# The first half of each stage-end norm in three operations per tile, from PSUM, with query norms ahead of the search

## The chip, the cores and the metric

The kernel runs on one core of a Trainium2 chip. The metric is the time of one execution on the device, in microseconds, as the median of several runs. The engines named below are TensorE (PE, with PEld for its weight loads), VectorE (DVE), ScalarE (ACT), GpSimd (POOL) and SyncE (SP, which only issues transfers here).

## What is computed

Two layers of a trunk, for a prompt of 512 tokens and 8 samples of 4 tokens, 544 columns in all, with 1024 channels:

```python
h  = rmsnorm(x, norm1) * (1 + sc1) + sh1          # shift, scale and gate: silu(c) @ w_ada + b_ada
q, k, v, qi, ki, wi, pool_u, z, xbc, dt, gates = split(h @ w_in)
q = rope(rmsnorm(q, q_norm), pos)                 # 16 heads of 64: the query norms
# attention over the 256 keys with the best indexer scores (the search), pooling, state-space scan
x = x + g1 * (merged @ w_out)
h2 = rmsnorm(x, norm2) * (1 + sc2) + sh2
a, g = split(causal_dwconv3(h2 @ ffn_up))
x = x + g2 * ((silu(g) * a) @ ffn_down)
```

The prompt has one shift and scale per channel, each sample its own. All in fp32.

## The kernel before

Channels lie on the 128 partitions (8 tiles `x[k]` of 128 x 544), tokens in the free dimension, in two halves of 272 columns; the samples are the last 32 columns of the second half. Each fp32 product runs as three fp32r products: weights and activations are split into a rounded part and a rest (`wh` and `wl`, `hh` and `hl`), and `wh*hh`, `wh*hl` and `wl*hh` are added up in PSUM. `weights` (L348) loads a 512 KB tile to `raw` over SP's queue, casts it to `wh` on ACT and subtracts to `wl` on VectorE (L357), all with a raised priority. `raw` has four buffers, `wh` and `wl` three each. `gemm` (L360) makes one such product with 48 matmuls (L371).

`gemm2` (L375) makes two products half by half (L388): both sources for the first 272 columns, then both for the rest. It is used at the three stage ends (layer 0's output projection to its FFN, layer 0's FFN to layer 1's projection, layer 1's output projection to its FFN). There `gemm_norm` (L472) makes the last two output tiles and calls `norm` after each half, while PE goes on to the other half; the next stage begins with `gemm2` as well, so that it can start on the half that is ready.

A norm half (`norm`, L397) squares on ACT (L428), adds up on VectorE (L430), takes the mean over channels with matmuls (L459), then eleven small VectorE operations (`newton`, L303, and two that add eps) for the inverse root `rstdh`; six matmuls (L468) spread it over the partitions, and a copy brings it to SBUF as `rb`. Then per tile: `hn = x * rb` (L434), `hn * gm + shift` (L444, ACT Identity), the cast to `hh` and the subtraction to `hl` (L452). For the first tile but one, the multiply and the last subtraction are on POOL (the sites nm1 and nl1), for the last tile the cast is on VectorE (nh7). In the second half the samples take two more POOL operations per tile (L449, L450).

Work of other chains is issued in steps: `pump` takes from each lane as many generator steps as its rate, once in each `gemm` and twice in `gemm2`. Lane a is `ada` (L246), the product of silu(c) with w_ada: in the start-up for layer 0's first third, in layer 0's pooling branch for the rest, and in layer 0's FFN for layer 1. Lane t is the search (`topk1`, L856), pairs of MAX8 and MATCH_REPLACE8 on VectorE. In `attention` (L1301) `qnorm` takes the inverse root of the query norms for two groups of four tiles, into the halves of `rq`; `qbc` (L1369) spreads a half for the sample tokens, and PE turns it in L1374. A planner (TileContext) orders each engine's instructions before the run, by their place in the program, the raised priorities and its own timing; the order is then fixed, and each engine follows its own list.

Of the kernel before, what the change touches and what calls it, by code (L numbers as in the profile page):

```python
# [23 lines left out]
F32 = mybir.dt.float32  # L24
F32R = mybir.dt.float32r
BF16 = mybir.dt.bfloat16
I32 = mybir.dt.int32
AF = mybir.ActivationFunctionType
OP = mybir.AluOpType
# [7 lines left out]
HC = T // 2  # L37
# [9 lines left out]
WPRI = 300  # L47
# [43 lines left out]
W_UP = 127  # L91
# [12 lines left out]
class Prog:  # L104
# [134 lines left out]
    def ada(self, l, s, first=False):  # L239

        nc, a = self.nc, self.a
        par, mod, _ = self.par[l]
        m0 = 16 * s
        pick = lambda x: x.rearrange("p (h c t) n -> p c h t n", h=2, c=4)
        dst = pick(mod[:, m0:m0 + 16, :])
        bias = par[:, P_BADA + m0:P_BADA + m0 + 16].rearrange("p (h c t) -> p c h t", h=2, c=4)  # L246
        turn = None
        for c in range(4):
            ps = self.P("ada1")
            for pair in range(2):  # L250
                raws = []
                for z in (2 * pair, 2 * pair + 1):
                    with self.tc.high_priority(offset=WPRI):
                        raw = self.wr.tile([128, 1024], F32, name="raw", tag="raw")
                        nc.sync.dma_start(raw, a["w_ada"][l, s, 4 * c + z])
                    raws.append(raw)
                    if z % 2 == 0:
                        yield

                prods = []  # L260
                for k4 in range(4):
                    prods.append(nc.tensor.matmul(ps[32 * k4:32 * k4 + 32, :], self.sc[:, 4 * pair + k4, :],
                                     raws[k4 // 2][:, (k4 % 2) * 512:(k4 % 2) * 512 + 512],
                                     start=(pair == 0), stop=(pair == 1)))
                if pair == 0:
                    if turn:
                        turn(prods[-1].ins)
                        turn = None
                    yield
            if turn:  # L270
                turn(prods[-1].ins)
            row = self.t("adarow")
            self.copy("ada2", row[:, :512], ps)
            turn = self.ada_turn(row, dst[:, c], bias[:, c], first)
            if first or c == 3:
                turn(None)
                turn = None
            yield
# [68 lines left out]

    def weights(self, src, n):  # L348
        nc = self.nc
        z = self.nw = (self.nw + 1) % 4  # L350
        with self.tc.high_priority(offset=WPRI):
            raw = self.wr.tile([128, 1024], F32, name="raw", tag="raw")
            nc.sync.dma_start(raw[:, :n], src)
            wh = self.wh.tile([128, 1024], F32R, name="wh", tag="wh")
            wl = self.wh.tile([128, 1024], F32R, name="wl", tag="wl")
            self.copy("weights2", wh[:, :n], raw[:, :n])
            self.last_wl = self.E("weights1").tensor_tensor(wl[:, :n], raw[:, :n], wh[:, :n].bitcast(F32), op=OP.subtract).ins  # L357
        return wh, wl
# [15 lines left out]

    def gemm2(self, srcs, rhs, done=None):  # L375

# [3 lines left out]
        K = len(rhs)  # L380
        ws, self.pre = self.pre or [self.weights(src, K * 128) for src in srcs], None
        os_ = [self.G() for _ in srcs]
# [14 lines left out]
    def norm(self, l, second, c, st):  # L397
        if c == 0:
            for k in range(0, 8, 2):
                self.norm_gm(l, second, st, k)  # L400
        self.norm_stats(c, st, self.nc.gpsimd)
        for k in range(8):
            self.norm_apply(l, second, c, st, k)

# [8 lines left out]

    def norm_stats(self, c, st, eng):
        nc = self.nc
# [10 lines left out]
        for k in range(8):  # L426
            q = st["q"][k] if k else sq[0]
            nc.scalar.activation(q[:, cs], self.x[k][:, cs], AF.Square)  # L428
            if k:
                (nc.vector if k >= NV else eng).tensor_tensor(sq[k % 2][:, cs], sq[1 - k % 2][:, cs], q[:, cs],  # L430
                                                              op=OP.add)
        self.norm_half(sq[1], c, rb)
        for k in range(8):
# [19 lines left out]

    def norm_half(self, sq, c, rb):
        nc = self.nc
# [11 lines left out]
        for i, (t0, w) in enumerate(blocks):  # L467
            nc.tensor.matmul(o[:, t0:t0 + w], r[:w, i:i + 1].to_broadcast([w, 128]), self.ident[:w, :w],  # L468
                             start=True, stop=True)
        self.copy("norm_half3", rb[:, c * HC:c * HC + HC], o[:, :HC])  # L470

# [117 lines left out]
    def project(self):  # L589
        nc, a, l = self.nc, self.a, self.l  # L590
        par, mod, _ = self.par[l]
        h = self.h
        o, ok = self.gemm2([self.w(l, W_KI), self.w(l, W_K)], h)
        kd, self.ki = self.t("kd"), self.t("ki")
# [706 lines left out]
    def attention(self):  # L1301
# [29 lines left out]
        def qnorm(sqs, c0):  # L1331
            mk = yield from self.ssq(sqs, "mq")
            self.newton(mk, self.s([128, 5, 8], "rsq_u8"), rq[:, :, c0:c0 + 8])
            yield
# [33 lines left out]
        for p in range(2):  # L1368
            self.E("attention7").tensor_copy(bc[p][:32, :512].rearrange("p (i e d) -> p i e d", i=4, e=2),  # L1369
                                  rq[:32, 4, 8 * p:8 * p + 8].rearrange("p (i e) -> p i e", e=2)[:, :, :, None]  # L1370
# [239 lines left out]
    def ffn(self):  # L1610
# [7 lines left out]
        for ci, n in enumerate(CH):  # L1618
            fs = []
            for jj in range(n):  # L1620
# [8 lines left out]
                if j == 0:  # L1629
                    o, o2 = self.gemm2([self.w(l, W_UP), self.w(l, W_UP + 1)], h)  # L1630
                else:
                    o = self.gemm(self.w(l, W_UP + 2 * j), h)
# [200 lines left out]
```

## Time and profile before

| what | value |
| --- | --- |
| median of 3 runs | 3163.01 us (3154.23, 3163.01, 3165.09) |
| the profiled execution | 3159.91 us, of which the span is 3158.1 us |
| mean granted clock of TensorE | 0.980 |
| PE busy | 3037.2 us (96%) |
| VectorE busy | 2235.4 us (71%) |
| ACT busy | 1261.9 us (40%) |
| POOL busy | 881.0 us (28%) |

Times in rows are microseconds from the span's start, unless they are marked ns. An idle time stands in brackets with what ended it. A row can stand for several instructions in a row of the same kind (x7). L numbers are lines of the kernel before. Matmul ends are modelled, and neighbours in one engine overlap a little, so that durations add up to somewhat more than the time they take.

### The profile page before, as it was taken

The numbers are of one execution on the slowest core, as the hardware profiler recorded it, in microseconds if no ns is written. First come the engines' busy times: TensorE is split into PE (matmuls) and PEld (weight loads), VectorE is DVE, ScalarE is ACT, GpSimd is POOL, SyncE is SP. The second block draws the span as 40 slices with busy tenths as digits, with TensorE's granted clock in tenths as the row PEclk, the third lists the DMA queues.
The fourth block names the chain that finished last, engine by engine and source line by source line (L and its number), as shares of the span: only waits on it lengthen the run. The fifth ranks groups of instructions, "written<-read, shape, count | busy, mean of one in ns | idle before, by whom it ended". The sixth has DMA issues, their size and how long they took to land. (4 is left out here: it accounts for less than half of the span.)

```text
span 3158.1 us, 62620 instructions
## 1 busy us (share of the span) xinstructions
PE 3037.2 (96%) x24136; PEld 2791.9 (88%) x24136; DVE 2235.4 (71%) x4879; ACT 1261.9 (40%) x2240; POOL 881.0 (28%) x1273
## 2 busy tenths in 40 slices
PE   7999999999999999999989999999999899999999
PEld 4987998999986789998989878989999857899999
DVE  5687878679988656454566878786799885564554
ACT  4344443333336534343443344343333364342432
POOL 1363445521121003111223635455211110121211
PEclk9999999999999999999999999999999899999999
DMA  6332332345543443545333323223333244333322
GB/s 234 107 110 75 113 95 99 113 137 185 190 125 122 162 143 102 162 153 170 94 117 107 107 78 116 93 90 123 99 132 116 79 136 152 98 90 90 86 97 76
DMA packets 303100, 376.81 MB, mean 119 GB/s; under 512 B 177362, under 2 KB 186930, under 8 KB 302802
## 3 DMA queue, kind: packets, MB, share of 16 engines
q1 hardware_dynamic: 116514, 315.94, 29.7%
q10 hardware_dynamic: 181216, 42.05, 6.6%
q0 software_dynamic: 5072, 14.83, 1.3%
q8 instruction: 190, 3.11, 0.4%
q14 instruction: 108, 0.88, 0.1%
HBM read 330.34 MB, written 33.79 MB: 115 GB/s over the span
## 5 line engine op out<-in xcount | busy, mean ns | idle before, releaser
L371 PE MATMUL psg<-hh,wh 128*128 128x272 f32 x4064 | 859.0, 291 | 9.1 <-ACT cacc L894 4.9
L177 ACT ACTIVATE wh<-raw 128x1024 fp32r<-128x1024 f32 (+2 forms) x434 | 425.0, 980 | 1107.1 <-PE psg L371 752.1
L371 PE MATMUL psg<-hl,wh 128*128 128x272 f32 x4064 | 850.0, 289 | 0.0
L371 PE MATMUL psg<-hh,wl 128*128 128x272 f32 x4064 | 847.6, 290 | 0.0
L357 DVE TENSOR_TENSOR wl<-raw,wh 128x1024 fp32r<-128x1024 f32 (+2 forms) x434 | 509.5, 1174 | 334.2 <-ACT wh L177 329.6
L371 PEld LDWEIGHTS psg<-hh,wh 128*128 128x128 f32 x4064 | 642.8, 190 | 35.4 <-issue 14.0
L371 PEld LDWEIGHTS psg<-hh,wl 128*128 128x128 f32 x4064 | 640.4, 189 | 9.8 <-issue 7.2
L371 PEld LDWEIGHTS psg<-hl,wh 128*128 128x128 f32 x4064 | 640.4, 190 | 6.8 <-issue 4.7
L896 POOL COPY sti<-cu 128x32 f32<-128x32 f32 x136 | 85.4, 628 | 522.7 <-ACT cu L177 522.5
L901 DVE SCALAR_TENSOR_TENSOR cacc<-cu,half,cacc 128x511 f32<-128x511 f32 x144 | 137.4, 954 | 5.9 <-ACT cacc L894 4.9
L910 ACT ACTIVATE th<-cacc 128x544 f32<-128x544 f32 x92 | 60.4, 656 | 199.7 <-DVE cacc L904 179.8
L371 PE MATMUL psg<-fh,wh 128*128 128x272 f32 x648 | 133.9, 290 | 2.6 <-DVE resid L495 2.6
L371 PE MATMUL psg<-fl,wh 128*128 128x272 f32 x648 | 133.7, 288 | 0.0
L371 PE MATMUL psg<-fh,wl 128*128 128x272 f32 x648 | 133.6, 288 | 0.0
L489 DVE SCALAR_TENSOR_TENSOR x<-psg,mod,x 128x272 f32<-128x272 f32 x64 | 32.0, 499 | 140.5 <-PE psg L371 131.4
L371 PE MATMUL psg<-oh,wl 128*128 128x272 f32 x512 | 110.1, 291 | 0.0
L371 PE MATMUL psg<-ol,wh 128*128 128x272 f32 x512 | 109.4, 291 | 0.0
L371 PE MATMUL psg<-oh,wh 128*128 128x272 f32 x512 | 109.3, 292 | 0.0
L371 PEld LDWEIGHTS psg<-fh,wh 128*128 128x128 f32 x648 | 100.8, 188 | 8.6 <-PE psg L371 3.4
L1638 POOL TENSOR_TENSOR cacc<-cacc 128x544 f32<-128x544 f32 x44 | 62.2, 1414 | 154.5 <-DVE cacc L911 154.5
L1041 POOL TENSOR_TENSOR seg<-seg,cb 128x512 f32<-128x512 f32 x64 | 89.9, 1407 | 52.5 <-ACT seg L1040 39.3
L911 DVE SCALAR_TENSOR_TENSOR cacc<-th,cacc 128x544 f32<-128x544 f32 x92 | 72.8, 792 | 42.7 <-ACT th L910 42.5
(481 smaller groups left out, 6180.0 us busy)
## 6 DMA issues: line engine op xcount, KB each, us to landing
raw<-wk SPq DMA_DIRECT2D x326, 512.0 KB, 3.3
raw<-w_ada SPq DMA_DIRECT2D x96, 512.0 KB, 4.3
h<-h SPq DMA_DIRECT2D x64, 256.0 KB, 4.5
raw<-wk SPq DMA_DIRECT2D x64, 256.0 KB, 2.8
o_ssds<-hn ACTq DMA_DIRECT2D x64, 256.0 KB, 2.1
raw<-wd SPq DMA_DIRECT2D x32, 448.0 KB, 3.4
kvr<-ckv SPq DMA_DIRECT2D x48, 256.0 KB, 4.0
kvw<-ckv SPq DMA_DIRECT2D x48, 256.0 KB, 3.9
```

Of the source, the lines that this page charges most:

```text
L177: self.nc.scalar.activation(out, src, AF.Copy)
L357: self.last_wl = self.E("weights1").tensor_tensor(wl[:, :n], raw[:, :n], wh[:, :n].bitcast(F32), op=OP.subtract).ins
L371: nc.tensor.matmul(o[:, c, :HC], w[:, k * 128:(k + 1) * 128], x[:, c * HC:(c + 1) * HC], start=(k == 0 and first), stop=(k == K - 1 and last))
L489: self.E("resid1").scalar_tensor_tensor(x[:, :HC], o[:, 0, :HC], g[:, 0:1], x[:, :HC], op0=OP.mult, op1=OP.add)
L896: self.E("conv1").tensor_copy(st[:, i, :, W - 1:], new)
L901: self.E("conv3").scalar_tensor_tensor(acc[:, s:512], u[:, :512 - s], wc, acc[:, s:512], op0=OP.mult, op1=OP.add)
L910: nc.scalar.activation(th, acc, AF.Tanh)
L911: self.E("silu21").scalar_tensor_tensor(acc, th, 1.0, acc, op0=OP.add, op1=OP.mult)
L1041: self.E("ssd_chain5").tensor_tensor(d[:, :512], d[:, :512], cb[:, :512], op=OP.mult)
L1638: self.E("ffn3").tensor_tensor(s_, s_, aa, op=OP.mult)
```

## The change

Four edits:

- `norm`, first half only: `norm_half` no longer copies to `rb` but returns the PSUM tile, the multiplies of `norm_stats` are left out, and `norm_direct` makes each tile in three operations: `u = x * gm * o` on VectorE from PSUM, `hi = u + shift` on ACT, `lo = (u + shift) - hi` on VectorE. It does the same for all eight tiles.
- `weights` can put the subtraction to `wl` on another engine; the two products that begin layer 1's projection and each FFN use POOL. (In layer 0's projection these weights are prepared earlier, on VectorE as before.)
- `ada` loads both tiles of a pair and only then yields, so that their matmuls come one step later than both loads.
- In `attention`, `newton` for the query norms and the copy to `qbc` have their priority raised by 600 places (twice WPRI).

```diff
@@ ada
                         nc.sync.dma_start(raw, a["w_ada"][l, s, 4 * c + z])
                     raws.append(raw)
-                    if z % 2 == 0:
-                        yield
+                yield
 
@@ weights, gemm2
-    def weights(self, src, n):
+    def weights(self, src, n, eng=None):
...
             self.copy("weights2", wh[:, :n], raw[:, :n])
-            self.last_wl = self.E("weights1").tensor_tensor(wl[:, :n], raw[:, :n], wh[:, :n].bitcast(F32), op=OP.subtract).ins
+            eng = eng or self.nc.vector
+            if eng is self.nc.gpsimd:
+                eng.tensor_tensor(wl[:, :n], raw[:, :n], wh[:, :n].bitcast(F32), op=OP.subtract)
+                return wh, wl
+            self.last_wl = eng.tensor_tensor(wl[:, :n], raw[:, :n], wh[:, :n].bitcast(F32), op=OP.subtract).ins
...
-        ws, self.pre = self.pre or [self.weights(src, K * 128) for src in srcs], None
+        ws, self.pre = self.pre or [self.weights(src, K * 128, eng) for src in srcs], None
@@ norm
-        self.norm_stats(c, st, self.nc.gpsimd)
+        o = self.norm_stats(c, st, self.nc.gpsimd, not c)
         for k in range(8):
-            self.norm_apply(l, second, c, st, k)
+            if c:
+                self.norm_apply(l, second, c, st, k)
+                continue
+            self.norm_direct(l, second, c, st, k, o)
+
+    def norm_direct(self, l, second, c, st, k, o):
...
+        sh = mod[:, b + k, 0:1]
+        nc.vector.scalar_tensor_tensor(u[:, ps], x[:, ps], gm[:, k, 0:1], o[:, :t1 - t0], op0=OP.mult, op1=OP.mult)
+        nc.scalar.activation(hi.bitcast(F32R)[:, ps], u[:, ps], AF.Identity, bias=sh)
+        nc.vector.scalar_tensor_tensor(lo.bitcast(F32R)[:, ps], u[:, ps], sh, hi[:, ps], op0=OP.add, op1=OP.subtract)
@@ norm_stats, norm_half
-        self.norm_half(sq[1], c, rb)
+        o = self.norm_half(sq[1], c, rb, direct)
+        if direct:
+            return o
...
-        self.copy("norm_half3", rb[:, c * HC:c * HC + HC], o[:, :HC])
+        if not direct:
+            self.copy("norm_half3", rb[:, c * HC:c * HC + HC], o[:, :HC])
+        return o
@@ project
-        o, ok = self.gemm2([self.w(l, W_KI), self.w(l, W_K)], h)
+        o, ok = self.gemm2([self.w(l, W_KI), self.w(l, W_K)], h, eng=nc.gpsimd)
@@ attention
             mk = yield from self.ssq(sqs, "mq")
-            self.newton(mk, self.s([128, 5, 8], "rsq_u8"), rq[:, :, c0:c0 + 8])
+            with self.tc.high_priority(offset=2 * WPRI):
+                self.newton(mk, self.s([128, 5, 8], "rsq_u8"), rq[:, :, c0:c0 + 8])
...
-            self.E("attention7").tensor_copy(bc[p][:32, :512].rearrange("p (i e d) -> p i e d", i=4, e=2),
+            with self.tc.high_priority(offset=2 * WPRI):
+                self.E("attention7").tensor_copy(bc[p][:32, :512].rearrange("p (i e d) -> p i e d", i=4, e=2),
@@ ffn
-                    o, o2 = self.gemm2([self.w(l, W_UP), self.w(l, W_UP + 1)], h)
+                    o, o2 = self.gemm2([self.w(l, W_UP), self.w(l, W_UP + 1)], h, eng=nc.gpsimd)
```

## Rows read from the trace of the kernel before

**Rows 1.** Part 1 of the page: busy time, share of the span, instructions.

```profile
PE 3037.2 (96%) x24136; PEld 2791.9 (88%) x24136; DVE 2235.4 (71%) x4879; ACT 1261.9 (40%) x2240; POOL 881.0 (28%) x1273
```

**Rows 2.** Waits of PE: who waited for whom; us in total, times, longest.

```profile
PE psb L1374 <- DVE qbc L1369: 9.5, 2, 8.6
PE psb L262 <- DMA raw<-w_ada: 9.0, 6, 4.5
PE psa L468 <- DVE rstdh L311: 8.5, 4, 3.8
```

**Rows 3.** The same list for the first 70 us alone.

```profile
PE psb L262 <- DMA raw<-w_ada: 2.9, 3, 2.1
```

**Rows 4.** Timeline of PE, second stage end: start, duration, operation, idle before.

```profile
1622.88 1.35 PE L468 MATMUL psa<-cst,rstdh 128*128 128x128 f32 x6 [3.80 <-DVE rstdh L311]
...
1627.33 0.82 PE L388 MATMUL psg<-hh,wh 128*128 128x272 f32 x2 [2.01 <-ACT hh L177]
```

**Rows 5.** Windows there: busy us per engine (instructions), granted clock, DMA share, GB/s.

```profile
1632.00:1636.00 4.00, 4.00 (x17) 3.83 (x17) 3.22 (x8) 1.47 (x4) 2.32 (x6) 0.50 0.00 0
...
1640.00:1644.00 4.00, 4.00 (x35) 4.00 (x34) 2.06 (x6) 0.88 (x3) 0.72 (x4) 1.00 0.00 0
```

**Rows 6.** Timeline of VectorE, second stage end, in order of time.

```profile
1616.81 1.23 DVE L357 TENSOR_TENSOR wl<-raw,wh 128x1024 fp32r<-128x1024 f32 x1 [0.22 <-ACT wh L177]
...
1620.12 1.23 DVE L357 TENSOR_TENSOR wl<-raw,wh 128x1024 fp32r<-128x1024 f32 x1
...
1622.66 0.16 DVE L311 SCALAR_TENSOR_TENSOR rstdh<-rsq_u,rstdh 128x3 f32<-128x3 f32 x1
1624.27 0.44 DVE L173 COPY rb<-psa 128x272 f32<-128x272 f32 x1 [1.45 <-PE psa L468]
1624.74 3.12 DVE L434 TENSOR_TENSOR hn<-x,rb 128x272 f32<-128x272 f32 x7
...
1629.83 0.65 DVE L309 TENSOR_TENSOR rsq_u<-rstdh 128x3 f32<-128x3 f32 x1
...
1632.78 0.44 DVE L173 COPY rb<-psa 128x272 f32<-128x272 f32 x1 [0.85 <-PE psa L468]
...
1640.80 1.85 DVE L452 TENSOR_TENSOR hl<-hn,hh 128x272 fp32r<-128x272 f32 x5
```

**Rows 7.** Timeline of ACT, second stage end.

```profile
1625.22 1.73 ACT L444 ACTIVATE hn<-hn,mod,gm 128x272 f32<-128x272 f32 x3 [4.81 <-DVE hn L434]
1626.86 0.41 ACT L177 ACTIVATE hh<-hn 128x272 fp32r<-128x272 f32 x1
```

**Rows 8.** Part 5 of the page: busy us, mean ns, idle before, what ended it.

```profile
L489 DVE SCALAR_TENSOR_TENSOR x<-psg,mod,x 128x272 f32<-128x272 f32 x64 | 32.0, 499 | 140.5 <-PE psg L371 131.4
```

**Rows 9.** Timeline of POOL, second stage end.

```profile
1629.69 0.77 POOL L452 TENSOR_TENSOR hl<-hn,hh 128x272 fp32r<-128x272 f32 x1 [3.89 <-ACT hh L177]
```

**Rows 10.** Instructions of L1638: duration in ns, least, median and most.

```profile
L1638 POOL TENSOR_TENSOR cacc<-cacc x44: 1340/1364/1869, 1206.8 to 3116.3; 128x544 f32<-128x544 f32 x44
```

**Rows 11.** Timeline of VectorE, then of PE, first stage end.

```profile
1170.02 0.15 DVE L311 SCALAR_TENSOR_TENSOR rstdh<-rsq_u,rstdh 128x3 f32<-128x3 f32 x1
...
1172.87 1.92 PE L262 MATMUL psb<-raw,sc 128*32 128x512 f32 x4 [4.47 <-DMA raw<-w_ada]
```

**Rows 12.** Timeline of VectorE, layer 1's query norms and search.

```profile
2470.05 0.17 DVE L311 SCALAR_TENSOR_TENSOR rq<-rsq_u,rq 128x40 f32<-128x40 f32 x1
...
2480.26 0.16 DVE L540 TENSOR_SCALAR mq<-psa 128x32 f32<-128x32 f32 x1
...
2491.83 0.81 DVE L1427 TENSOR_TENSOR qs<-q,qs 64x128 fp32r<-64x128 f32 x3
...
2493.85 0.20 DVE L311 SCALAR_TENSOR_TENSOR rq<-rsq_u,rq 128x40 f32<-128x40 f32 x1
```

**Rows 13.** Timeline of PE in the same stretch.

```profile
2485.89 1.91 PE L1374 MATMUL psb<-cst,qbc 32*128 32x32 f32 x8 [8.55 <-DVE qbc L1369]
```

**Rows 14.** Window in the same stretch, columns as in rows 5.

```profile
2480.00:2490.00 10.00, 4.11 (x18) 4.05 (x19) 9.97 (x31) 0.00 (x0) 1.03 (x4) 0.50 0.33 88
```

More of the change, by code (lines that the diff above doesn't have):

```diff
@@ L373, in gemm, with gemm2 @@
         return o
-    def gemm2(self, srcs, rhs, done=None):
+    def gemm2(self, srcs, rhs, done=None, eng=None):
         nc = self.nc
@@ L400, in norm @@
                 self.norm_gm(l, second, st, k)
-        self.norm_stats(c, st, self.nc.gpsimd)
+        o = self.norm_stats(c, st, self.nc.gpsimd, not c)
         for k in range(8):
-            self.norm_apply(l, second, c, st, k)
+            if c:
[3 more added lines that the diff above has]
+    def norm_direct(self, l, second, c, st, k, o):
+        nc = self.nc
+        _, mod, _ = self.par[l]
+        b = 24 if second else 0
+        gm, u, x = st["gm"], st["us"][k], self.x[k]
+        hi, lo = st["hi"][k], st["lo"][k]
+        t0, t1 = c * HC, min(c * HC + HC, 512)
+        ps = slice(t0, t1)
+        sh = mod[:, b + k, 0:1]
+        nc.vector.scalar_tensor_tensor(u[:, ps], x[:, ps], gm[:, k, 0:1], o[:, :t1 - t0], op0=OP.mult, op1=OP.mult)
+        nc.scalar.activation(hi.bitcast(F32R)[:, ps], u[:, ps], AF.Identity, bias=sh)
+        nc.vector.scalar_tensor_tensor(lo.bitcast(F32R)[:, ps], u[:, ps], sh, hi[:, ps], op0=OP.add, op1=OP.subtract)
     def norm_gm(self, l, second, st, k):
@@ L412, in norm_gm, with norm_stats @@
                                             op0=OP.add, op1=OP.mult)
-    def norm_stats(self, c, st, eng):
+    def norm_stats(self, c, st, eng, direct=False):
         nc = self.nc
@@ L452, in norm_apply, with norm_half @@
         self.E("nl%d" % k).tensor_tensor(lo.bitcast(F32R)[:, cs], u[:, cs], hi[:, cs], op=OP.subtract)
-    def norm_half(self, sq, c, rb):
+    def norm_half(self, sq, c, rb, direct):
         nc = self.nc
```

## The prediction

> **What bounds the kernel now.** Part 1 of the page comes first: TensorE (PE) is busy in 96% of the span [rows 1], so only what idles PE, or halves its clock, can move the time. The second view is PE's list of waits: the reader looks there for waits that come seldom and are long. Three belong to this change [rows 2]: 9.5 us in two waits for the tile qbc (query norms), 9.0 us for the loads of w_ada and 8.5 us for rstdh, the Newton result of a stage-end norm. Of the 9.0 us, 2.9 fall in the first 70 us [rows 3]. The third view is one stage end in windows and in time, here layer 0's FFN to layer 1's projection. The other two (1152 to 1200 and 2727 to 2768) have the same pattern. PE ends the old stage at 1619.08 (1622.88 less 3.80 of idle), waits for the Newton chain, runs six matmuls of L468, and waits another 2.01 us for the first hh [rows 4]. The idle time also costs clock: 17 matmuls in 4 us at a granted 0.50 (the lower level, 1.2 GHz) against 35 in 4 us at 1.00 (2.4 GHz) [rows 5].
>
> So a stage end has three legs: up to the Newton result (rstdh), from there to the first hh, and then whichever is slower, PE's 96 matmuls or the second half's norm, whose last hl ends at 1640.80 + 1.85 = 1642.65 [rows 6].
>
> **Norm of the first half, direct from PSUM.** Removed per half: one copy to rb (0.44), eight multiplies (seven on VectorE in 3.12, one on POOL), eight ACT Identity operations (1.73 for three, 0.58 each), eight casts (0.41 each, one on VectorE) and eight subtractions (1.85 for five, 0.37 each) [rows 6, 7]. Added per tile: u on VectorE with one operand in PSUM, priced by the residual's operation of the same form, 0.50 [rows 8]; hi on ACT, between a cast's 0.41 and an Identity's 0.58; lo on VectorE, not in the trace, between 0.37 (hl) and 0.50 (the other three-operand form). I take 0.42, nearer hl, as neither input is in PSUM.
>
> From the last L468 matmul, about 1624.23, the first hh now takes rb, multiplies and several Identity operations, and PE starts at 1627.33 [rows 4, 7]. Afterwards it is 0.50 + 0.58 + some 0.1 of hand-over, near 1625.4: 1.9 us earlier. But VectorE does not get lighter. It had 0.44 + 3.12 + 7 x 0.37 + some 0.3 = 6.5 us per half; it will have 8 x (0.50 + 0.42) = 7.4, or 8 x (0.42 + 0.37) = 6.3 where neighbours overlap as the seven multiplies do. ACT drops from 7.5 to about 4 us. Today VectorE runs the second half's Newton chain while it waits for ACT's casts; afterwards u and lo leave no such hole, and the chain (eleven operations at 0.20 pitch, 2.2 us) comes behind them. The second half's rb, which ends at 1633.22, 9.0 us after L468 [rows 6], would come some 6.3 + 2.2 + 1.6 (L468 again) + 0.44 = 10.5 us after it. In return no first-half hl stands among the second half's multiplies. What is late next is therefore the second half's chain. I credit 1 us of the 1.9 (bounds -1 and 1.9).
>
> **The subtraction wl on POOL.** Six of them move, two per stage end. Today each costs VectorE 1.23 us, and the second sits inside the Newton chain, at 1620.12 [rows 6]. If nothing else happened, rstdh would be ready about 2.2 us earlier (at 1620.6 instead of 1622.82): both subtractions are in front of it, less what the add and x wait for anyway. On POOL none has 1024 columns in this trace. From 0.77 for 272 columns and 1.36 for 544 [rows 9, 10] the slope is 2.2 ns a column and I estimate 2.4 us. The Trainium skill (GPSIMD Engine Reference, 2.1 Instruction dispatch) states about 2.5 cycles an element for two inputs, which at its 1.2 GHz would be an estimate of 2.1 us; the sum does not use it.
>
> The price is not POOL's time: a wl is first needed after hh. The price is a collision that the trace shows. A Newton step at 1629.83 took 0.65 us instead of 0.16, and ended at 1630.48, just when POOL's hl (1629.69 + 0.77 = 1630.46) ended [rows 6, 9]. So a small VectorE operation with two SBUF inputs sat out the POOL operation. Two POOL subtractions at the old places (from 1616.8 and from 1620.1) would end at 1619.2 and 1622.5. A Newton chain begun behind the first has some 0.9 us before the second, then waits, and does its last eight steps after 1622.5, up to 1624.3: 1.5 us later than today. Bounds for rstdh: 2.2 earlier, 1.5 later. I take 1.0 later, near the collision of [rows 6, 9], because both subtractions start when the chain does. With the 1 us above, a stage end comes to 0 (bounds -2.5 and 4.1), the three to 0.
>
> The Trainium skill (SBUF — State Buffer, section on SBUF's two separate sides) says that VectorE and GpSimd share one port pair as an exclusive lock, held for the whole instruction, against VectorE operations with two SBUF inputs; it speaks against this edit. By that, the trace agrees (0.65 against 0.16); with the rule in every stage end the sum would be 1 us a stage end worse than mine, without it about 3 us better.
>
> **The loads of w_ada.** The generator now loads both tiles of a pair in one step and multiplies in the next; counts of loads and matmuls stay. At the first stage end rstdh was ready at 1170.17, but PE stood 4.47 us at a w_ada matmul queued in front of L468, until four of its matmul records (1.92 us) could start at 1172.87 [rows 11]. With the pair loaded a step ahead this wait should go; the matmuls remain. Behind it comes rstdh itself. I take 4 us (bounds 0 and 6.1, all such waits after the first 70 us) [rows 2, 3]. In the first 70 us the waits are 2.9 us, but there the loads follow one another anyway: I take 1 (0 to 2.9). What it costs: SP's queue now has two w_ada loads in front of a weight load, which lands later. I cost that at nothing, since the list of PE's waits names no weight tile of any size; the cover is the weight that was split one product earlier. Should it go, each of 40 pairs pays (16 in the pooling branch, 24 in the FFN of layer 0).
>
> **Query norms in front of the search.** The change raises the eleven Newton steps and the qbc copy, not the two operations of L540 and L544 ahead of them. In layer 1 the first four heads' Newton ends at 2470.22, yet PE waits 8.55 us for their qbc until 2485.89, with a clock of 0.50 in that stretch and VectorE full (9.97 of 10 us) [rows 12 to 14]. The copy can move to the front. What is late next: the second Newton, begun behind L540 at 2480.26 and ended at 2494.05, for the second qbc, and qs for the next scores, ended at 2492.64 [rows 12]. PE, let go at 2477.3, has some 8.6 us of work before it needs them, so it arrives near 2486 and waits again, unless the raised Newton is done in one piece by 2483. The gain lies between 0 and 13.5 us (the 9.5 of waits, and some 4 of half clock over this and the next stretch). I take 7. The search steps that are passed are wanted only by the sample attention further on. In layer 0 no such wait is in the list: nothing.
>
> **The sum.** 0 + 4 + 1 + 7 = 12 us. The profiled execution took 3159.9 us (span 3158.1, under 2 around it); the three runs have a mean of 3160.8 and a median of 3163.0, so it lies with their mean. 3160.8 - 12 = 3148.8, and from the profiled one 3147.9: I forecast 3148.
>
> **Rivals.** *The collision misses the Newton chain*: the instruction order, or POOL itself, puts the subtractions beside operations that don't mind. For it: u, with an operand in PSUM, and the first two Newton steps have one SBUF input. Then each stage end gives 2.2 + 1, some 9.6 in all, and the query norms about 9: 3160.8 - 9.6 - 5 - 9 = 3137. *The waits only move*: PE meets the second Newton and qs as late as now, because search and Newton steps already alternate one for one and a raised priority cannot break into a running 1.2 us search step, and a w_ada pair is again drawn in front of L468. Query norms 2, loads 1, stage ends 0: 3158. This is also the case in which the change does not do what it says. *Slower, by the stage ends*: the subtractions and the Newton chain run one after the other in full, and the second half's Newton is queued behind all sixteen u and lo. It decides from the point where rstdh comes over 1.9 us later than now (after 1624.7 in the stage end shown), since the direct form has no more to give. With rstdh 2.5 later and the second half's chain another 2, three stage ends lose 13, and with nothing from query norms and 1 from loads it is 3173. The skill's lock rule, applied to every one of the six subtractions, leads here.
>
> **How the numbers follow.** Chances: forecast 0.45 (its own range 3141 to 3155), collision missed 0.18, waits only move 0.23, slower 0.14. The 80% range leaves out most of the slower case and the best third of the missed collision: 3134 to 3166. About 0.3% (9.5 us) is what a measurement of this kernel tells from no change, so faster means below 3151 and slower above 3170. Faster: 0.33 of the forecast's 0.45, 0.18, and 0.01 of the third: 0.52. Slower: 0.12. The same: 0.36.
>
> **What would show it.** Right: no PE wait over 2 us for qbc; the first hh some 1.2 us after L468; Newton steps of over 1 us beside wl on POOL; PE's wait before L468 not shorter than 3.6 us in the second and third stage end; no w_ada wait over 1 us after the first 70 us. Wrong: PE waits for wh or wl in the stretches with w_ada loads; PE idle between the two halves of a new stage, which would make the second half's norm the bound; a new wait at L1433 as long as the old one at L1374.

## The result and the profile after

The changed kernel takes 3175.33 us (median of 7 runs), the kernel before in the same comparison 3160.73 us. The ratio is 1.0054 with a 95% interval of 1.0038 to 1.0070: slower by 17 us (12 to 22). The forecast was 3148. The profiled execution of the changed kernel took 3171.93 us.

The first view is the page's busy time and PE's list of waits, which answer to [rows 1, 2]. Columns: us in total, times, longest us.

```profile
PE 3040.6 (96%) x24136; PEld 2797.3 (88%) x24136; DVE 2237.5 (71%) x4873; ACT 1251.6 (39%) x2219; POOL 891.2 (28%) x1273
...
PE psb L1400 <- DVE qbc L1395: 12.7, 3, 6.1
PE psb L261 <- DMA raw<-w_ada: 10.1, 8, 4.4
PE psg L391 <- ACT hh L177: 9.9, 3, 3.6
PE psa L490 <- DVE rstdh L310: 9.8, 3, 5.1
...
PE psg L391 <- DVE hl L423: 4.0, 2, 2.0
```

None of the three waits that the change aims at got shorter: qbc 12.7 us (9.5 before), w_ada 10.1 (9.0), rstdh 9.8 (8.5). One is new, for the first hl of a stage, 2.0 us, twice. Now the second stage end on PE, as [rows 4], with the first qbc of layer 0 ahead of it:

```profile
921.28 3.62 PE L1400 MATMUL psb<-cst,qbc 32*128 32x32 f32 x16 [6.10 <-DVE qbc L1395]
...
1626.29 1.76 PE L490 MATMUL psa<-cst,rstdh 128*128 128x128 f32 x6 [5.06 <-DVE rstdh L310]
...
1629.20 0.82 PE L391 MATMUL psg<-hh,wh 128*128 128x272 f32 x2
1632.03 0.60 PE L391 MATMUL psg<-hl,wh 128*128 128x272 f32 x1 [2.02 <-DVE hl L423]
...
1638.46 0.92 PE L490 MATMUL psa<-cst,rstdh 128*128 128x128 f32 x6
...
1643.38 0.82 PE L391 MATMUL psg<-hh,wh 128*128 128x272 f32 x2 [3.05 <-ACT hh L177]
...
1646.59 0.60 PE L391 MATMUL psg<-hl,wh 128*128 128x272 f32 x1 [0.96 <-POOL hl L474]
```

The six matmuls of L490 are those of L468 in the kernel before: they spread the inverse root over the partitions. The wait for the first hh is gone, and one of the same length for the first hl (2.02) stands in its place. The second half's spreading matmuls (L490 at 1638.46) come late, and PE then idles 3.05 + 0.96 us between the two halves, where it did not stop before. VectorE in the same stretch, as [rows 6]; in the rows of the first half u is the tile hn (L421), hi is hh and lo is hl (L423):

```profile
1620.19 2.45 DVE L305 TENSOR_SCALAR rsq_u<-msh 128x3 int32<-128x3 int32 x1
...
1624.13 1.22 DVE L360 TENSOR_TENSOR wl<-raw,wh 128x1024 fp32r<-128x1024 f32 x1
...
1626.08 0.16 DVE L310 SCALAR_TENSOR_TENSOR rstdh<-rsq_u,rstdh 128x3 f32<-128x3 f32 x1
1628.09 3.35 DVE L421 SCALAR_TENSOR_TENSOR hn<-x,gm,psa 128x272 f32<-128x272 f32 x8 [1.85 <-PE psa L490]
...
1631.50 2.13 DVE L423 SCALAR_TENSOR_TENSOR hl<-hn,mod,hh 128x272 fp32r<-128x272 f32 x5
1633.56 0.15 DVE L305 TENSOR_SCALAR rsq_u<-msh 128x3 int32<-128x3 int32 x1
1633.63 1.31 DVE L423 SCALAR_TENSOR_TENSOR hl<-hn,mod,hh 128x272 fp32r<-128x272 f32 x3
...
1636.62 0.16 DVE L310 SCALAR_TENSOR_TENSOR rstdh<-rsq_u,rstdh 128x3 f32<-128x3 f32 x1
1639.42 0.44 DVE L173 COPY rb<-psa 128x272 f32<-128x272 f32 x1 [2.64 <-PE psa L490]
```

And POOL beside it:

```profile
1620.23 2.38 POOL L358 TENSOR_TENSOR wl<-raw,wh 128x1024 fp32r<-128x1024 f32 x1
```

All eight u run first, then the lo, and ten of the second half's eleven Newton operations behind the last lo. The second half's rb ends at 1639.86, 11.8 us after the first half's spreading matmuls (1626.29 + 1.76 = 1628.05); before it was 9.0 [rows 4, 6].

To see where time goes over the whole program, the start of the same PE matmul is compared in two traces. The matmul that starts at 1593.91 in the kernel before starts at 1596.14 in the changed one, 2.2 us later; the one at 1660.56 starts at 1669.21, 8.6 later: the stretch between, with the second stage end, lost 6.4 us. PE idles 12.05 us in it, 7.24 before, so 4.8 of the 6.4 are idle time. The rest is clock: after the stop the second half's matmuls run at the lower level again (granted 0.50 from 1643 to 1652), where the kernel before held 1.00 from 1637 to 1652. In this way, in us (plus is lost against before; the numbers in the head are starts in the kernel before; the ratio is to the kernel before of the same comparison):

| kernel | ratio, 95% interval | query norms layer 0, 801 to 943 | stage end 1, 1147 to 1213 | FFN layer 0, 1213 to 1594 | stage end 2, 1594 to 1661 | query norms layer 1, 2450 to 2531 | stage end 3, 2723 to 2774 |
| --- | --- | --- | --- | --- | --- | --- | --- |
| changed | 1.0054, 1.0038 to 1.0070 | 9.7 | -2.9 | -1.7 | 6.4 | -3.5 | 6.0 |
| e1_loads | 1.0001, 0.9988 to 1.0014 | 9.0 | 0.6 | -1.7 | 0.2 | -1.5 | 0.0 |
| e2_wl | 0.9985, 0.9971 to 0.9999 | 2.0 | -7.7 | 2.3 | 1.3 | -1.3 | 0.8 |
| e3_direct | 1.0050, 1.0036 to 1.0064 | 2.7 | 6.3 | 6.2 | 5.6 | -0.1 | 6.0 |
| e4_query | 1.0005, 0.9988 to 1.0021 | 0.0 | 0.2 | 5.0 | 0.6 | -6.4 | 0.1 |
| f1_turns | 1.0034, 1.0022 to 1.0047 | 3.2 | 1.7 | 2.5 | 3.5 | -3.5 | 3.8 |
| f2_newton | 1.0012, 1.0000 to 1.0025 | 2.3 | 2.0 | 7.0 | 0.3 | -1.7 | 1.9 |
| f3_both | 1.0019, 1.0007 to 1.0032 | 2.6 | -0.2 | 1.1 | 2.5 | -2.7 | 2.5 |
| f4_after_no_loads | 1.0066, 1.0048 to 1.0085 | 2.4 | 1.6 | 1.6 | 7.2 | -0.4 | 6.0 |
| g1_no_direct | 0.9997, 0.9986 to 1.0007 | 8.9 | -8.4 | -1.7 | 0.9 | -0.4 | 0.2 |
| g2_search_behind | 1.0062, 1.0041 to 1.0082 | -1.7 | -0.1 | 3.8 | -0.2 | -11.7 | -0.8 |
| g3_wl_search | 1.0043, 1.0028 to 1.0057 | -0.1 | -7.8 | 3.8 | 1.3 | -13.2 | -0.1 |
| g4_wl_first | 0.9984, 0.9973 to 0.9994 | 3.1 | -5.6 | 6.3 | 0.6 | -1.4 | 0.0 |

The ratios come from several executions, the stretches from one each. How far a stretch scatters by itself is told by kernels that list its instructions as the kernel before does. At the third stage end that is little: e1_loads and g4_wl_first show 0.0. In the FFN of layer 0 it is much. The ten kernels without the w_ada edit have there, on PE, VectorE, ACT and POOL, the order of the kernel before, and take 1.1 to 7.0 us longer than its trace. PE idles 2.2 to 5.8 us in them (1.3 in the kernel before), most of it for w_ada, for the ada row that ACT copies (adarow) and for ACT's fh. So I put no figure of that column down to those edits. The columns are not the whole, either: up to 130 us, start-up moved by -4.8 to +3.1 us in the same ten kernels, in which it has the order of the kernel before.

### The profile page after: what moved, and what is told of

It reads as the page before. It is cut to its first block, busy times and chain, and to the rows that moved or that the text cites. A ratio compares the mean times of both kernels' runs of the same rounds, so it can differ in the third digit from the quotient of the medians.

```text
span 3170.1 us, 62606 instructions
## 1 busy us (share of the span) xinstructions
PE 3040.6 (96%) x24136; PEld 2797.3 (88%) x24136; DVE 2237.5 (71%) x4873; ACT 1251.6 (39%) x2219; POOL 891.2 (28%) x1273
## 5 line engine op out<-in xcount | busy, mean ns | idle before, releaser
L360 DVE TENSOR_TENSOR wl<-raw,wh 128x1024 fp32r<-128x1024 f32 (+2 forms) x428 | 501.5, 1172 | 324.5 <-ACT wh L177 319.4
L374 PEld LDWEIGHTS psg<-hh,wh 128*128 128x128 f32 x4064 | 642.4, 189 | 32.3 <-issue 17.9
L374 PEld LDWEIGHTS psg<-fh,wl 128*128 128x128 f32 x648 | 101.2, 188 | 1.7 <-issue 0.8
```

What stands on the lines that cost most here:

```text
L360: self.last_wl = eng.tensor_tensor(wl[:, :n], raw[:, :n], wh[:, :n].bitcast(F32), op=OP.subtract).ins
L374: nc.tensor.matmul(o[:, c, :HC], w[:, k * 128:(k + 1) * 128], x[:, c * HC:(c + 1) * HC], start=(k == 0 and first), stop=(k == K - 1 and last))
```

## The experiments

**One edit at a time.** Four kernels are the kernel before with one part of the change each.

```diff
 e1_loads, in ada:
-                    if z % 2 == 0:
-                        yield
+                yield
```

> The kernel before with the w_ada edit alone. Theory A (the loads' order moves the search in layer 0): PE again stands some 6 us at the first qbc of layer 0, its first project gains 2.3 us at start-up, and the whole is 3 to 6 us slower than before, near 3165. Theory B (the raised query norms do that): no such wait here, the w_ada waits shrink, and the whole is 2 to 5 us faster, near 3157.

The wait is there (4.54 us at the first qbc of layer 0), and the stretch loses 9.0 us, so theory A has the place right. The whole was not slower: 1.0001. Why the stretch loses is seen on VectorE at the search's start in this kernel:

```profile
782.29 0.68 DVE L861 MATCH_REPLACE8 wk<-mx,wk 128x512 f32<-128x512 f32 x1
785.00 0.31 DVE L290 TENSOR_REDUCE adat<-psb 128x36 f32<-128x144 f32 x1 [2.03 <-PE psb L287]
785.92 1.23 DVE L356 TENSOR_TENSOR wl<-raw,wh 128x1024 fp32r<-128x1024 f32 x1 [0.62 <-ACT wh L177]
787.06 0.69 DVE L860 MAX8 mx<-wk 128x8 f32<-128x512 f32 x1
787.67 1.20 DVE L860 MAX8 mxs<-wks 32x8 f32<-32x1028 f32 x1
```

In the kernel before, the search for the samples (mxs) starts at 773.68 and its rounds alternate with the last rounds of another search (mx). Here the mx rounds stand alone, VectorE idles 2.03 us for the reduction of an ada row, and mxs starts at 787.67. PE is 4.2 us later here, so VectorE is some 9.7 us further behind PE. It is 85 to 99% busy in every 20 us from 780 to 920 and does not catch up before the norms. The changed kernel shows the same (781.96, with PE 1.4 us earlier); so do all three kernels with this edit, and none of the ten without it: their stretch loses at most 3.2. That the later search causes the loss is read from this order; no edit moved the search back alone.

```diff
 e2_wl, in gemm2 (weights as in the change):
-        ws, self.pre = self.pre or [self.weights(src, K * 128) for src in srcs], None
+        ws, self.pre = self.pre or [self.weights(src, K * 128, eng) for src in srcs], None
```

> The kernel before with the subtraction to wl on POOL for the products at the stage ends, alone. Theory C (POOL's subtraction holds up VectorE's small operations): rstdh comes 1 to 2 us later in the second and third stage ends, with a VectorE operation of about 2.4 us beside it, and the whole is 2 to 5 us slower. Theory D (the order of the direct norm costs the stage ends, not POOL): rstdh within 0.5 us of before, the whole within 1.5 us of before.

Theory C was right on the mechanism and wrong on the time. In the first stage end VectorE and POOL show:

```profile
1150.04 2.37 DVE L502 TENSOR_TENSOR x<-x,resid 128x32 f32<-128x32 f32 x1
...
1160.59 2.40 DVE L434 TENSOR_TENSOR sqa<-sqb,sqx 128x272 f32<-128x272 f32 x1 [0.54 <-ACT sqx L432]
```

```profile
1149.97 2.40 POOL L359 TENSOR_TENSOR wl<-raw,wh 128x1024 fp32r<-128x1024 f32 x1 [20.87 <-ACT wh L177]
1160.32 2.38 POOL L359 TENSOR_TENSOR wl<-raw,wh 128x1024 fp32r<-128x1024 f32 x1 [7.95 <-ACT wh L177]
```

An addition of 32 columns that takes 0.19 us elsewhere took 2.37, and ended (1152.41) where POOL's subtraction did (1152.37). The second, of 272 columns, takes 0.44 elsewhere; it took 2.40 and ended at 1162.99, 0.29 behind POOL's. In the other stage ends the wait for rstdh grew from 3.80 to 5.04 and from 3.61 to 4.09. Yet the first stage end got 7.7 us cheaper: L472 now stands ahead of the ada matmuls in PE's list, and the 4.47 us at w_ada [rows 11] are gone. The whole is 0.9985, faster by 4.7 us (0.3 to 9.2).

```diff
 e3_direct, in norm (norm_direct as in the change):
-        self.norm_stats(c, st, self.nc.gpsimd)
+        o = self.norm_stats(c, st, self.nc.gpsimd, not c)
...
+            self.norm_direct(l, second, c, st, k, o)
```

> The kernel before with the direct norm of the first half alone. Theory D (VectorE makes all eight u before any lo, and the second half's Newton chain comes behind them): PE stops between the halves for over 3 us in the second and third stage ends, each 4 to 7 us slower than before, the whole 8 to 13 us slower. Theory C (POOL's subtraction is what costs the stage ends): the halves follow without a stop, each stage end gains 1 to 2 us, and the whole is 3 to 5 us faster.

Theory D: 1.0050, some 16 us, and 6.3, 5.6 and 6.0 us at the three stage ends. PE in the second one shows the pattern of the changed kernel, and no subtraction to wl runs on POOL here:

```profile
1637.74 1.76 PE L487 MATMUL psa<-cst,rstdh 128*128 128x128 f32 x6 [3.80 <-DVE rstdh L311]
...
1643.47 0.59 PE L388 MATMUL psg<-hl,wh 128*128 128x272 f32 x1 [2.02 <-DVE hl L420]
...
1656.00 0.82 PE L388 MATMUL psg<-hh,wh 128*128 128x272 f32 x2 [3.05 <-ACT hh L177]
...
1659.22 0.59 PE L388 MATMUL psg<-hl,wh 128*128 128x272 f32 x1 [0.97 <-POOL hl L471]
```

```diff
 e4_query:
+            with self.tc.high_priority(offset=2 * WPRI):
+                self.newton(mk, self.s([128, 5, 8], "rsq_u8"), rq[:, :, c0:c0 + 8])
...
+            with self.tc.high_priority(offset=2 * WPRI):
+                self.E("attention7").tensor_copy(bc[p]...)
```

> The kernel before with the raised priority of the query norms alone. Theory A (the loads' order costs layer 0): layer 0 as before, the wait at the first qbc of layer 1 falls from 8.6 to some 6 us, and the whole is 3 us faster, near 3158. Theory B (the priority costs layer 0): PE stands some 6 us at the first qbc of layer 0, which costs 8 to 10 us there against 3 gained in layer 1: near 3167.

Layer 0 is as before, so the priority does not cost it anything. The wait in layer 1 fell to 5.6 us, but not because the norms overtook the search. VectorE in this kernel:

```profile
2483.00 0.16 DVE L540 TENSOR_SCALAR mq<-psa 128x32 f32<-128x32 f32 x1
...
2484.37 1.20 DVE L862 MATCH_REPLACE8 wks<-mxs,wks 32x1028 f32<-32x1028 f32 x1
2485.50 0.16 DVE L306 TENSOR_SCALAR rsq_u<-mq 128x40 int32<-128x40 int32 x1
2485.60 1.22 DVE L861 MAX8 mxs<-wks 32x8 f32<-32x1028 f32 x1
2486.75 0.16 DVE L307 TENSOR_SCALAR rq<-rsq_u 128x40 int32<-128x40 int32 x1
...
2486.93 1.20 DVE L862 MATCH_REPLACE8 wks<-mxs,wks 32x1028 f32<-32x1028 f32 x1
2488.07 0.18 DVE L309 TENSOR_TENSOR rsq_u<-rq 128x40 f32<-128x40 f32 x1
2488.17 0.41 DVE L1371 COPY qbc<-rq 32x512 f32<-32x512 f32 x1
```

The kernel before has the same operations in the same order, each 2.7 us earlier: L540 at 2480.26 [rows 12], qbc at 2485.43. The raised Newton steps still alternate with search steps; of what was raised only the copy for the second qbc moved, by two places. PE came 6.5 us late into this stretch and left it on time, because VectorE and not PE sets its end there. The lateness (5.0 us of it from the scatter in layer 0's FFN) was taken up, and the whole is 1.0005. In e3_direct, where VectorE is as late as PE (both by some 19 us), nothing is taken up (-0.1).

**The order in the direct norm.** Three kernels start from e3_direct and change only the order of its operations.

```diff
 f1_turns, in norm_direct:
+        los = st.setdefault("los", [])
+        with self.tc.issue_after(los[k - 2]) if k > 1 else nullcontext():
             nc.vector.scalar_tensor_tensor(u[:, ps], x[:, ps], gm[:, k, 0:1], o[:, :t1 - t0], op0=OP.mult, op1=OP.mult)
...
```

> The direct norm alone (as in the run of that edit), but with u and lo in turns: u of tile k+2 is queued behind lo of tile k. If PE's 2.0 us wait for the first hl comes from all eight u standing before the first lo, it falls below 0.5 us in the second and third stage ends and each gets 1.5 to 2 us cheaper than with the direct norm alone. If the second half's Newton chain is what costs most, PE's stop between the halves stays or grows by as much as the first half gained, and the whole is within 3 us of the direct norm alone, near 3178 if before is at 3162.

The wait for the first hl is gone, and the second and third stage ends are cheaper by 2.1 and 2.2 us (5.6 to 3.5, 6.0 to 3.8). PE's stop between the halves grew from 3.05 to 4.00 us in the second one. The whole is 1.0034, some 5 us better than e3_direct: the first stage end gained as well (6.3 to 1.7).

```diff
 f2_newton, in norm_direct, and in norm_stats behind the second half's norm_half:
+        def low():
...
+        if k < 2:
+            low()
+        else:
+            st.setdefault("late", []).append(low)
...
+        for f in st.pop("late", []):
+            with self.tc.issue_after(self.last_newton):
+                f()
```

> The direct norm alone, but with the lo of tiles 2 to 7 queued behind the second half's Newton chain. If that chain behind u and lo is the cause of PE's stop between the halves, the second half's rb comes some 8.5 us after the first half's spreading matmuls (12.6 with the direct norm alone, 9.0 before), the stop of 3 to 4 us plus 1 us for hl goes, the wait of 2.0 us for the first hl stays, and each stage end gets 3 to 4 us cheaper: the whole some 10 us faster than the direct norm alone, 1.001 to 1.003 of before. If the stop has another cause (ACT, POOL), it stays.

This removed most of the loss: 1.0012, and 2.0, 0.3 and 1.9 us at the stage ends in place of 6.3, 5.6 and 6.0. PE in the second one:

```profile
1631.68 1.76 PE L497 MATMUL psa<-cst,rstdh 128*128 128x128 f32 x6 [3.81 <-DVE rstdh L311]
...
1637.42 0.60 PE L389 MATMUL psg<-hl,wh 128*128 128x272 f32 x1 [2.02 <-DVE hl L422]
...
1640.31 1.44 PE L497 MATMUL psa<-cst,rstdh 128*128 128x128 f32 x6
...
1649.42 0.40 PE L389 MATMUL psg<-hl,wh 128*128 128x272 f32 x1 [1.67 <-POOL hl L481]
```

The second half's rb ends at 1642.65, 9.2 us after the first L497 (9.0 before, 13.0 in e3_direct), and the stop for hh is gone. What is late next is POOL's hl of the second tile, behind that half's operations for the samples. My figure of 8.5 us was 0.7 too low.

```diff
 f3_both: both orders, five lo ahead of the chain
+        if k < 5:
+            los.append(low().ins)
+        else:
+            st.setdefault("late", []).append(low)
```

> The direct norm alone with both: u and lo in turns for the first five tiles, then the second half's Newton chain, then the last three lo. If the two orders are the whole cause, neither the wait for the first hl (2.0 us) nor the stop between the halves (3 to 4 us and 1 us) is left, and the gain that the direct form promised shows: the second and third stage ends 1 to 2 us cheaper than before, the whole 0.999 to 1.000 of before. If VectorE's work is too much in any order, one of the two waits stays over 1.5 us.

The last sentence came true: rb ends 9.0 us after the first half's spreading matmuls, as before, but waits of 1.81 us (hh) and 1.68 us (POOL's hl) stay, and the two stage ends lose 2.5 us each. The first half starts earlier, but no order that was tried brings the second half earlier than in the kernel before. In e3_direct and these three kernels the three stage ends together give about the whole: 17.9, 9.0, 4.2 and 4.8 us, against 16, 11, 4 and 6 by the ratios.

**Parts left out, and the search moved for good.**

```diff
 f4_after_no_loads, from the changed kernel, in ada:
-                yield
+                    if z % 2 == 0:
+                        yield
```

> The changed kernel without the w_ada edit (the other three parts stay). If the loads' order costs layer 0's query norms some 9 us, PE does not wait for qbc in layer 0, and the whole is 4 to 9 us faster than the changed kernel, near 3166 if before is at 3161. If the loss in layer 0 belongs to the priority together with the rest, the wait stays and the time is that of the changed kernel or above.

The wait in layer 0 is gone (0.81 us) and the stretch cheaper by 7.2 us, but the whole is 1.0066, no faster than the changed kernel. What the w_ada edit costs at the query norms it gave back elsewhere: without it the first stage end is dearer by 4.5 us, the FFN by 3.3 and layer 1's query norms by 3.1 (one trace each).

`g1_no_direct` is the changed kernel with `norm` as in the kernel before.

> The changed kernel without the direct norm (the w_ada edit, POOL's subtraction and the raised query norms stay). If the direct norm is what makes the change slower, this is within 0.15% of before, 0.998 to 1.0015, and the stage ends have no stop between the halves. If the parts only hurt together, it stays above 1.003.

0.9997: with the other three parts alone nothing is lost. PE runs from half to half without a stop, and the second and third stage ends lose 0.9 and 0.2 us. The direct norm is the cause of the slower result.

```diff
 g2_search_behind, from the kernel before:
-TR = (2, 1, 3, 1, 0)
+TR = (2, 1, 3, 0, 0)
```

> The kernel before with one number changed: the lane of the search takes no step during the eight query products, so that its last steps come behind the query norms in the program and not by a priority. If PE's wait for qbc in layer 1 is VectorE's search standing in front, 8.6 us falls below 2 us and the whole is 6 to 12 us faster, 0.996 to 0.998, unless the sample attention then waits for its mask. If the wait only moves to the mask or to qs, the whole is within 3 us of before.

The first half came true: no wait for qbc is left, and layer 1's query norms are cheaper by 11.7 us. But the whole is 1.0062. Twelve search rounds now stand among the attention's operations, and the 200 us behind them lose 20. PE's waits in this kernel (in the kernel before 2.6 us for PT, 1.9 for S and none of L1456 for anb):

```profile
PE psb L1461 <- ACT PT L177: 9.3, 15, 0.8
...
PE psa L1456 <- DVE S L1445: 7.4, 9, 2.3
...
PE psa L1456 <- DVE anb L1441: 3.8, 2, 2.0
```

And its windows behind the query norms (columns: us, then PE, PEld, DVE, ACT, POOL busy with counts, granted clock, DMA share, GB/s):

```profile
2520.00:2540.00 20.00, 18.86 (x143) 16.94 (x143) 19.55 (x65) 8.39 (x27) 2.11 (x8) 1.00 0.56 171
2540.00:2560.00 20.00, 13.14 (x58) 7.73 (x57) 19.43 (x73) 9.47 (x28) 2.17 (x8) 0.68 0.11 41
2560.00:2580.00 20.00, 15.65 (x123) 9.47 (x122) 15.62 (x55) 8.66 (x26) 1.06 (x4) 0.67 0.00 1
```

VectorE is full (19.55 and 19.43 of 20 us), PE falls to 13.14 busy, and the granted clock to 0.68, a mean of time at 2.4 and at 1.2 GHz. PE ran only 58 matmuls in the first of the two slow windows. In layer 0 the picture is the same: VectorE has 19.43 and 19.53 of 20 us from 940 to 980, and the granted clock falls to 0.75 and 0.59 from 960 to 1000.

`g3_wl_search` is e2_wl with the edit of g2_search_behind.

> POOL's subtraction and the search behind the query norms, without the other parts. If the two gains are in different places and add up, 0.994 to 0.997 of before. If either was only the planner's other order, the sum is smaller than the parts.

1.0043: the gain at the first stage end (7.8 us) and at layer 1's query norms (13.2) are both there, and so is the loss in the attention of both layers.

```diff
 g4_wl_first, from e2_wl:
-        o, ok = self.gemm2([self.w(l, W_KI), self.w(l, W_K)], h, eng=nc.gpsimd)
+        o, ok = self.gemm2([self.w(l, W_KI), self.w(l, W_K)], h)
...
-                    o, o2 = self.gemm2([self.w(l, W_UP), self.w(l, W_UP + 1)], h, eng=nc.gpsimd)
+                    o, o2 = self.gemm2([self.w(l, W_UP), self.w(l, W_UP + 1)], h, eng=None if l else nc.gpsimd)
```

> POOL's subtraction for the first stage end alone (layer 0's FFN); the other two keep it on VectorE. If the gain of that edit lies in the first stage end (7.7 us in its trace) and the other two lose 1 us each to the longer VectorE operations beside it, this is 1 to 3 us faster than POOL's subtraction at all three, 0.997 to 0.9985. If the gain is spread or is only the planner's other order, it is at 0.9985 to 1.0.

0.9984: the gain lies in the first stage end (5.6 us in the trace), and the others are as before (0.6 and 0.0). Against e2_wl (0.9985) no difference can be measured. These two are the fastest kernels here, ahead of both kernels compared; against the kernel before their margin is 0.3 to 9.2 and 1.9 to 8.5 us.

## Why the prediction was wrong

**The step that failed is the credit for the direct norm**, 1 us a stage end (bounds -1 and 1.9). Alone it costs 6.3, 5.6 and 6.0 us (e3_direct), and without it the rest of the change loses nothing (g1_no_direct). The sign of being wrong that I had set for it came: PE idle between the two halves. Three things in that step were wrong.

- *The first hh is not what PE needs.* I let PE go at the first hh and put lo beside it. The first hh matmul did come 1.15 us after L490 (1629.20 against 1628.05; 1.2 was said), but after two matmuls PE wants the first hl, and that stands behind all eight u: 1631.50 + 0.43 = 1631.93. The 2.01 us of [rows 4] moved from hh to hl. f1_turns shows that the order alone does this.
- *The second half's chain was sized too small, and not compared with when PE needs it.* I said 10.5 us from L490 to rb and took it for a fair trade. It was 11.8: u and lo took 6.9 (6.3 was said), and L490 of the second half is also late in PE's own list: Newton ended at 1636.78, and the matmuls started at 1638.46. And the cover was not worked out: I set the second half's norm against all 96 matmuls of PE, but PE needs it after the first 48, those of the first half. In the kernel before, ACT finished the second half's first hh at 1636.39 (first line: two of them from 1635.98, 0.41 us the first), and PE turned to that half at 1639.73:

```profile
1635.98 0.89 ACT L177 ACTIVATE hh<-hn 128x272 fp32r<-128x272 f32 x2
```

```profile
1639.73 0.41 PE L388 MATMUL psg<-hh,wh 128*128 128x272 f32 x2
```

ACT in the changed kernel:

```profile
1640.38 2.63 ACT L466 ACTIVATE hn<-hn,mod,gm 128x240 f32<-128x240 f32 x5 [8.34 <-DVE hn L456]
1642.92 0.41 ACT L177 ACTIVATE hh<-hn 128x272 fp32r<-128x272 f32 x1
```

The kernel before has a cover of 3.3 us. Counted from the end of the first half's spreading matmuls (1624.23 before, 1628.05 after), hh was ready 12.2 us and wanted 15.5 us after it; in the changed kernel it is ready 15.3 (1643.33) and wanted 12.3 (1640.33, which is 1643.38 less the idle 3.05). The cover of 3.3, less 3.1 and 3.2, is -3.0, which is the stop of 3.05 us. Of the 3.2, 1.9 is the earlier start (1.15 us behind the spreading matmuls, 3.1 before) and 1.3 a shorter run: the first half's 48 matmuls took 11.1 us in place of 12.4, the wait for hl included, since the granted clock rose to 1.00 some 6.9 us after the spreading matmuls and not 12.9. I had left that out as well. Even my own terms, rb 1.5 later and PE 1.9 earlier, would have used it up.
- *What follows rb* was left out: five Identity operations run before the first cast, and POOL's hl behind its operations for the samples (0.96, and 1.67 once the rest is mended).

**The subtraction on POOL** was the better part of the change, and the term was nearly right where it was looked at. I said 2.4 us for the operation (2.38), Newton steps of over 1 us beside it (2.45 against 0.17), and rstdh 1.0 later (1.2 and 0.5 in e2_wl, by PE's wait; 1.3 in the changed kernel). But I took both subtractions at the second stage end for those that move. Only one meets the chain; the other ran 9 us earlier (in e2_wl 1600.13 and 1609.34), and the wl at 1624.13 on VectorE belongs to the next product and stays inside the chain, as at 1620.12 before [rows 6]. I did not see at all that the first stage end would gain: I had given it the pattern of the other two, though PE stood there for w_ada and not for rstdh [rows 11].

I had written that the first two Newton steps and operations with one SBUF input do not mind POOL. The step that sat POOL out was the first of them, with one int32 input. The Trainium skill (SBUF — State Buffer, section SBUF: two separate sides) names VectorE operations in a 2-port performance mode beside those with two SBUF inputs; the trace agrees that the operation waits for POOL's whole instruction (it ended at 1622.64, POOL's at 1622.61), and no run here shows which of its modes this step ran in.

**The loads of w_ada**: 4 us credited at the first stage end. There the changed kernel has the wait behind the norm, 4.43 us at 1193.81, and e1_loads alone changes the stage end by 0.6 us. What gained there was POOL's subtraction (e2_wl, -7.7). The 1 us at start-up can't be told from the scatter: the first product after it comes 2.3 us earlier in the changed kernel and 5.2 later in e1_loads. "Nothing" for what the edit costs was wrong in kind. No weight came late, as said (no wait for wh or wl is in the list), but the planner listed VectorE's search otherwise, and layer 0's query norms lost 9 us, for which I had no term and no rival. What the edit was made for it does in layer 0's FFN, where most of the 24 pairs for layer 1 run and where I credited nothing: PE idles 0.7 us there in each of the three kernels with it, and 1.3 to 5.8 (3.9 in the mean) in the eleven traces without it. Over the whole program the edit comes to nothing (1.0001; and 1.0066 without it against 1.0054).

**The query norms**: 7 us credited in layer 1; the changed kernel gained 3.5, and by another way. "The copy can move to the front" failed. With the priority the order on VectorE is what it was (e4_query). The waits for qbc there, 8.55 and 0.92 us, became 5.92 and 0.72 since PE is 7.6 us late as it comes into that stretch, and the qbc matmul is only 4.2 late. f1_turns, without the priority, gains the same 3.5, and g1_no_direct, with it, 0.4. And "the search steps that are passed are wanted only by the sample attention further on" failed in a deeper way: g2_search_behind did put them behind, and lost 16 and 20 us in the two layers, as VectorE is full there as well.

**The rivals.** "Slower, by the stage ends" gave 3173, near the 3175 measured, and its second half, the second Newton behind all u and lo, is what happened. Its first half did not: rstdh came 1.3 us later, not over 1.9, and in e3_direct not later at all, with nearly the same loss. So the nearness of its number is in part luck: it has the three stage ends lose 13 us, where the trace shows 9.5 (-2.9, 6.4 and 6.0) and another 9.7 at layer 0's query norms, which it does not name. Of "the waits only move", its two ways were right for query norms and loads, but not its price.

**The sum.** Forecast: 0 for three stage ends, -5 for loads, -7 for query norms, -12 in all. By single edits: direct norm +16, POOL's subtraction -5, loads and priority within 2 of nothing, together some +13, against +17 (12 to 22) measured.

What stays open: why the same order in layer 0's FFN runs with 1.3 us of PE idle in one trace and 5.8 in another (by chance, or by when the stretch is entered: one trace of each kernel can't tell); why the w_ada edit moves the search in the planner's list; and whether any order of the direct norm beats the kernel before, since f3_both, the last one tried, still waits for hh and for POOL's hl.

## What to carry to other kernels

A shorter chain to the first tile is worth nothing if the second operand or the second half comes later: work out, for each consumer, when its input is ready and when it is wanted. The time between the two is its cover, and a delay costs what exceeds it (3.3 us of cover against 3.1 later and 3.2 earlier wanted, a stop of 3.05). Where one engine runs two chains in a fixed order, a chain without gaps can lose by holding up the one that is wanted next, which ran in the gaps before; f2_newton got back most of a 16 us loss by order alone. Where an engine is full, putting one of its users in front moves the wait to another user, and it can grow on the way (in g2_search_behind 9.5 us of waits for qbc went, and some 36 us were lost behind them).

## What the runs showed of the hardware that was not expected

- A VectorE addition of 128x32 (0.19 us) and one of 128x272 (0.44) took 2.37 and 2.40 us beside a POOL subtraction of 2.4 us (e2_wl), and a one-input int32 step on 128x3 took 2.45 in place of 0.17 (changed kernel). They ended 0.04, 0.29 and 0.03 us behind POOL's operation, so the price of such a meeting was nearly POOL's whole time, not that of the small operation.
- A stretch that VectorE bounded cost twice. In g2_search_behind PE was busy 28.8 of the 40 us from 2540 to 2580, and its granted clock fell from 1.00 to 0.68 and 0.67, so that the matmuls that did run were slower (those of L1456 378 ns in the mean, 291 before); the kernel before held 1.00 in the windows from 2520 to 2580.
